# A hybrid encoder step: four gate columns regrouped into two seven-product units, and attention's side work moved between engines

## The chip, the cores and the metric

The kernel runs on one core of a Trainium2 chip. The core has TensorE (matrix products, PE in the profile), VectorE (DVE), ScalarE (ACT), GpSimd (POOL), SyncE (SP, which here issues most of the transfers) and 16 DMA engines. The metric is device time in microseconds for one launch; the time before is the median of three runs.

## The reference

One encoder layer is computed for 1024 prompt tokens and 32 sample tokens, so 1056 in all, at width 1024. The parts that matter here:

```
h = RMSNorm(x)
z = h @ W_in -> [q_A | k_A | v_A | q_B | f_B | i_B | og_B | gate_A | gate_B]
A: sliding-window attention over chunks of 64 frames, 16 query heads, 2 kv heads of width 64,
   a sink logit for each head, a shared relative-position bias
B: gated linear recurrence (HGRN2), 8 heads, key and value width 128
m = sigmoid(gate_A) * (y_A @ W_brA) + sigmoid(gate_B) * (y_B @ W_brB)
x = x + RMSNorm(m @ W_out)
x = x + ConvFFN(RMSNorm(x));  x = x + (p @ W_ple) * sigmoid(x @ W_ple_gate)
```

gate_A and gate_B are 1024 columns each, so 16 columns of 128 (the kernel's column), each a product of all 1056 tokens with a 1024 x 128 slice of W_in. Nothing in the mathematics says when they are computed: they are needed only in m.

## The kernel before

**Precision.** Every large product works on pairs. A value is split into a rounded high part and a low part, the rest. Three matmuls (high x high, high x low, low x high) are added up in PSUM; that is `product`, lines 200 to 202. A weight column of 1024 x 128 is loaded into a `wr` tile, and `load_next` makes `wh` and `wl` of it (lines 181 to 184). The list `hi_on` says whether ScalarE or VectorE makes the high part.

**A column.** The tokens lie in three groups of 384, 384 and 288 (`GR`). `unit(out)` gives three blocks of one column, one for each group, 24 matmuls each. `stream(blocks, small)` runs blocks one after the other in two halves of 12 matmuls, and after half number m it emits the small work that is filed under m in the dictionary `small`. `gate_out` puts a tanh on the finished block (line 292) and stores it to DRAM (`ta_d`, `tb_d`). `next_w` prepares weights two columns ahead of their use; the order of all columns is the list `plan`.

**Who sets the order.** A scheduler in the framework orders each engine's instructions with the program's order as priority. Work whose inputs or buffers are not ready in its planning is overtaken by later work. `pinned` and `behind` tie a piece of work to what its engine has been given last. Each engine, and each of the queues of SP and GpSimd, then runs strictly in that order.

**The stages around the change.**

- *Start.* The tokens are normalised, transposed and split into `La` and `Lb` (high and low part of h).
- *Attention* (`stream(blocks, small)` behind the loop over i). Eight pairs of query heads, i from 0 to 7, called head 1 to 8 here. For each, 9 token tiles j run through `scores` (line 451 on: matmuls with q and k, the sum with the bias and the minimum on VectorE, line 457, the exponential on ScalarE, line 462, the scaling by the reciprocal on VectorE, line 466), `turn` (transposition on TensorE, line 478, and a split, lines 223 and 224) and `values` (matmuls with v, lines 500 and 501; two copies by ScalarE and two adds by VectorE bring the high and low halves together, lines 507 to 510). A small copy by GpSimd (line 455) puts the sink into the score tile before the exponential. There are five score tiles. The blocks under which this small work lies are those of 11 gate columns and of q for the next head pair: 57 blocks. `GB_AT` says with which heads the first three columns of gate_B go. `h_sums` adds up halves of h for the recurrent stage (lines 516 to 528) and stores them from GpSimd's queue. `cache_parts` loads the cached keys and values and splits them.
- *Between.* One gate column, `tb_d[3]`, in a stream of its own, while the sums of h come back (`TL`, `TH`).
- *Recurrent stage.* Eight heads with two units each: q and f, i and the output gate. A unit computes two columns at once with seven block products instead of eight for the 768 tokens of the first two groups (a Strassen-Winograd scheme: the four quarters of two weight columns and the halves of h are added up first, `b_parts`, and the products are combined afterwards, `e0` to `e10`), and directly for the third group. These are 11 pieces of 12 matmuls (lines 1006 to 1009): seven at 384 tokens and four at 288. `b_raw` loads two columns, `b_prepare` makes the parts (lines 931 to 944) three pieces ahead. The work of a head (`decay`, `factors`, `tile_in`, `tile_out`, `group_out`) is filed under the pieces with `at(m, ...)`; a head's tiles run under the next head's pieces.
- *Gate columns 5 to 8 of gate_B.* The list `tail`, 12 blocks. Eight of them run with the last head's tiles; the other four in the next stage, with the first loads of attention's output.
- *First branch product.* `load_split` loads attention's output from `ya_d` in 32 pieces and splits it into `Ra` and `Rb` (line 1340, 223, 224). Then 8 columns with 4 blocks of 264 tokens each follow (line 1380 for the evictions). After it come the second branch product, W_out, the ConvFFN and the last product, which the change leaves alone.

`back` reloads the parts of h whose memory the recurrent stage had taken; `more` lets the preparation of later columns begin. Both are filed under the last pieces of the recurrent stage.

Of the kernel before, what the change touches and what calls it, by code (L numbers as in the profile page):

```python
# [10 lines left out]
F32 = mybir.dt.float32  # L11
# [48 lines left out]
def layer_kernel(  # L60
# [83 lines left out]
    GA = [in_cols(5376 + c * P) for c in range(8)]  # L144
    GB = [in_cols(6400 + c * P) for c in range(8)]
    GB_AT = (0, 3, 7)
    for i in range(8):
        plan.append(GA[i])
        if i in GB_AT:
            plan.append(GB[GB_AT.index(i)])  # L150
        if i < 7:
            plan.append(in_cols((i + 1) * P))
    plan.append(GB[3])
    n_first = len(plan)
    plan += GB[4:]
# [17 lines left out]
    def load_next():  # L173
# [6 lines left out]
        if hi_on[0] == "act":  # L180
            S.copy(hi[:], raw[:])  # L181
        else:
            V.tensor_copy(hi[:], raw[:])
        V.tensor_tensor(lo[:], raw[:], hi[:].bitcast(F32), op=ALU.subtract)  # L184
        ready.append((hi, lo))

    hi_on = ["act"]
# [124 lines left out]
    with right("ap") as ap:  # L312
# [73 lines left out]

        def cache_parts():
            ck = ap.tile([P, P], F32, tag="kr", name="ck", bufs=2)
            dma(ck[:], flat(cache_win_k))
            t = tr_bank()  # L390
            E.transpose(t[:, 0:P], ck[:], ident[:])
            kt_ = ap.tile([P, GMAX], F32, tag="kt", name="ckt", bufs=2)
            S.copy(kt_[:, 0:P], t[:, 0:P])
            k_parts(kt_[:, 0:P], 1024, P)
            cv_ = ap.tile([P, P], F32, tag="kr", name="cv", bufs=2)
            dma(cv_[:], flat(cache_win_v))
            v_parts(cv_[:], P, 8)
# [45 lines left out]
        def scores(i, j):  # L443
# [21 lines left out]
            for h in range(2):  # L465
                V.tensor_scalar(sc[:m_, h, b0:e_], sc[:m_, h, b0:e_], st[:m_, 1, h:h + 1], None,
                                op0=ALU.mult)
# [21 lines left out]
        def values(i, js):  # L489
# [13 lines left out]
            u = aq.tile([P, 2, P], F32, tag="u", name=nm("u"), bufs=2)  # L503
# [3 lines left out]
            S.copy(u[0:64, :nx, :m_], o4[64:128, :, 0, :])  # L507
            S.copy(u[64:128, :nx, :m_], o4[0:64, :, 1, :])
            V.tensor_tensor(y3[0:64], o4[0:64, :, 0, :], u[0:64, :nx, :m_], op=ALU.add)
            V.tensor_tensor(y3[64:128], o4[64:128, :, 1, :], u[64:128, :nx, :m_], op=ALU.add)  # L510
# [3 lines left out]
        def h_sums(k):  # L514
# [3 lines left out]
            b11, b12, b21, b22 = (t[:] for t in hs)  # L518
            for t, (g, k_) in zip(hs, ((0, k), (1, k), (0, k + 4), (1, k + 4))):
                V.tensor_tensor(t[:], La[g][k_].bitcast(F32), Lb[g][k_].bitcast(F32), op=ALU.add)  # L520
            for part, t in zip(h_d, (La, Lb)):
                dma(part[:, k, :], t[1][k].bitcast(F32))
            V.tensor_tensor(b11, b11, b12, op=ALU.subtract)
            V.tensor_tensor(b12, b12, b22, op=ALU.subtract)
            V.tensor_tensor(b22, b22, b11, op=ALU.add)
            V.tensor_tensor(b21, b21, b22, op=ALU.subtract)
            for j, b in enumerate((b22, b12, b11, b21)):
                gdma(t_d[j][:, k, :], b)

# [9 lines left out]
        with tc.tile_pool(name="np", bufs=1, side="right", reuse_waits="tile") as np_:  # L539
# [267 lines left out]
            for k in range(2, 8):  # L807
# [8 lines left out]
                if k == 3:  # L816
                    load_raw()
                if k == 5:
# [26 lines left out]
        blocks, small = [(lambda w=w: w, 2, out) for w, out in zip(ws, outs)], {}  # L845
        for i in range(8):
            lo_ = 2 * len(blocks) if i else 0
            blocks += unit(gate_out(ta_d[i]))
            if i in GB_AT:
                blocks += unit(gate_out(tb_d[GB_AT.index(i)]))  # L850
            if i < 7:
                blocks += unit(q_out(i + 1))
            hi_ = 2 * len(blocks) - (6 if i == 7 else 0)
            if i == 0:
# [6 lines left out]
                small.setdefault(28, []).append(lambda: hi_on.__setitem__(0, "dve"))  # L861
            if i < 7:
                small.setdefault(lo_ + 2, []).insert(0, lambda i=i: bias_load(i + 1))
            for m, k in {0: ((16, 0), (22, 1)), 3: ((4, 2), (12, 3))}.get(i, ()):
                small.setdefault(lo_ + m, []).append(lambda k=k: pinned(lambda: h_sums(k), V))
# [1278 lines left out]
```

## Time and profile before

| | us |
|---|---|
| median of the runs shown (lowest to highest) | 2001.23 (2001.19 to 2003.25) |
| the profiled execution | 2002.58 |
| its span, first to last instruction | 2000.8 |
| TensorE busy in the span | 1984.3 |
| VectorE busy | 1424.5 |
| ScalarE busy | 965.4 |
| GpSimd busy | 228.4 |

The span is what the profile's rows add up to; the 1.8 us around it belong to the execution but to no instruction. Matmuls overlap each other, so a matmul's own duration is longer than its share of TensorE's time; the distance from one start to the next is what counts. "L200" is line 200 of the kernel. In a row of a group, the shape, the count, the busy time and the mean duration in ns of one are followed by the idle time of the engine just before these instructions and by what ended it. In a row of a stretch stand, for each engine, the busy time and in brackets the number of instructions, in the order PE, PEld (weight loads of TensorE), DVE, ACT, POOL, and then the granted clock of TensorE, the mean busy share of the DMA engines and GB/s.

### The profile page before, as it was taken

To read this page: it belongs to the slowest core of one execution; us is meant where nothing else is said; L and a number is where in the kernel's file an instruction comes from. 1 tells how busy PE (TensorE), PEld (TensorE's weight loads), DVE (VectorE), ACT (ScalarE), POOL (GpSimd) and SP (SyncE) were. 2 spreads that over 40 slices of the span, in tenths; PEclk is the share of its full clock that TensorE was granted. 3 is DMA by queue.
4 is the path that set the end of the run, shared out by engine and by line. 5 is a ranking of instruction groups with operands and counts; after the bars stand their busy time and mean duration, and the time that the engine had idled before them with its cause. 6 is when DMAs were issued, how large, how long until landed. Compare 5 with 4: busy or idle time off the path is not lost.

```text
span 2000.8 us, 37359 instructions
## 1 busy us (share of the span) xinstructions
PE 1984.3 (99%) x14304; PEld 1955.0 (98%) x14304; DVE 1424.5 (71%) x3138; ACT 965.4 (48%) x2159; POOL 228.4 (11%) x323
## 2 busy tenths in 40 slices
PE   8999999999999999999999999999999999999998
PEld 7899999999999999999999999999999999999998
DVE  6788888688888888554455788788888784655552
ACT  7555566566666666442124663333333344444432
POOL 1110100000000000002001023333333210000000
PEclk9999999999999999999999999999999999999999
DMA  7622311411111111377558582222222245655543
GB/s 257 155 92 85 106 53 55 154 43 58 58 37 51 41 54 54 123 241 220 166 165 291 173 288 70 80 76 86 76 86 76 86 141 195 213 192 173 171 130 80
DMA packets 253639, 247.47 MB, mean 124 GB/s; under 512 B 13893, under 2 KB 221912, under 8 KB 253461
## 3 DMA queue, kind: packets, MB, share of 16 engines
q1 hardware_dynamic: 245141, 218.59, 35.3%
q0 software_dynamic: 8240, 26.44, 3.7%
q8 instruction: 112, 1.84, 0.4%
q14 instruction: 66, 0.54, 0.1%
q10 hardware_dynamic: 80, 0.07, 0.0%
HBM read 177.56 MB, written 65.32 MB: 121 GB/s over the span
## 4 chain that ended last, share of the span: by engine, by line
PE 92%; DVE 4%; ACT 2%; DMA 1%; issue 1%; POOL 0%; SPq 0%; DVEq 0%; ACTq 0%; POOLq 0%
PE mm L200 14%; PE mm L201 14%; PE mm L202 14%; PE st L1867 7%; PE st L1866 7%; PE st L1865 7%; PE G L1009 2%; PE Y L1006 2%; PE G L1008 2%; PE G L1006 2%; PE Y L1009 2%; PE Y L1008 2%; PE tr L478 1%; PE X L1006 1%; PE so L1200 1%; PE X L1009 1%
## 5 line engine op out<-in xcount | busy, mean ns | idle before, releaser
L1865 PE MATMUL st<-op,wt 128*128 128x264 f32 x1232 | 348.6, 283 | 2.0 <-DVE Sp L1878 1.3
L1867 PE MATMUL st<-op,wt 128*128 128x264 f32 x1232 | 349.8, 284 | 0.0
L1866 PE MATMUL st<-op,wt 128*128 128x264 f32 x1232 | 347.6, 282 | 0.0
L184 DVE TENSOR_TENSOR wl<-wr,wh 128x1024 fp32r<-128x1024 f32 x129 | 157.9, 1224 | 120.7 <-ACT wh L181 111.7
L1865 PEld LDWEIGHTS st<-op,wt 128*128 128x128 f32 x1232 | 231.2, 188 | 3.5 <-DVE Sp L1878 1.7
L1866 PEld LDWEIGHTS st<-op,wt 128*128 128x128 f32 x1232 | 231.4, 188 | 0.0
L1867 PEld LDWEIGHTS st<-op,wt 128*128 128x128 f32 x1232 | 230.9, 187 | 0.0
L181 ACT CAST wh<-wr 128x1024 fp32r<-128x1024 f32 x116 | 121.8, 1050 | 197.7 <-PE mm L201 136.1
L200 PE MATMUL mm<-La,wh 128*128 128x384 f32 (+1 forms) x528 | 174.4, 331 | 0.0
L201 PE MATMUL mm<-Lb,wh 128*128 128x384 f32 (+1 forms) x528 | 170.9, 324 | 0.6 <-DVE Lb L710 0.6
L200 PE MATMUL mm<-ac,wh 128*128 128x352 f32 x528 | 170.8, 323 | 0.0
L202 PE MATMUL mm<-La,wl 128*128 128x384 f32 (+1 forms) x528 | 170.5, 323 | 0.2 <-DVE wl L685 0.2
L202 PE MATMUL mm<-ac,wl 128*128 128x352 f32 x528 | 169.8, 322 | 0.0
L201 PE MATMUL mm<-ac,wh 128*128 128x352 f32 x528 | 169.3, 321 | 0.0
L1625 ACT CAST wt<-wu 128x512 fp32r<-128x512 f32 x126 | 77.9, 619 | 186.6 <-POOL ab L1851 88.3
L200 PE MATMUL mm<-Ra,wh 128*128 128x264 f32 x512 | 145.4, 284 | 0.0
L201 PE MATMUL mm<-Rb,wh 128*128 128x264 f32 x512 | 145.0, 283 | 0.0
L202 PE MATMUL mm<-Ra,wl 128*128 128x264 f32 x512 | 145.0, 283 | 0.0
L1626 DVE TENSOR_TENSOR wt<-wu,wt 128x512 fp32r<-128x512 f32 x126 | 103.0, 820 | 39.0 <-ACT wt L1625 39.0
L462 ACT ACTIVATE sc<-sc,st 128x257 f32<-128x257 f32 (+1 forms) x144 | 69.7, 485 | 74.0 <-DVE st L457 73.0
L201 PEld LDWEIGHTS mm<-Lb,wh 128*128 128x128 f32 x528 | 99.4, 188 | 1.7 <-DVE Lb L710 1.4
L202 PEld LDWEIGHTS mm<-La,wl 128*128 128x128 f32 x528 | 99.2, 188 | 0.7 <-DVE wl L685 0.5
(496 smaller groups left out, 5694.8 us busy)
## 6 DMA issues: line engine op xcount, KB each, us to landing
wr<-in_w_down_dram SPq DMA_DIRECT2D x66, 512.0 KB
wu<-in_w_up_dram SPq DMA_DIRECT2D x42, 512.0 KB
wu<-in_w_in_dram SPq DMA_DIRECT2D x32, 512.0 KB
wr<-in_w_in_dram SPq DMA_DIRECT2D x25, 512.0 KB
ac<-act_d SPq DMA_DIRECT2D x66, 176.0 KB
act_d<-Up SPq DMA_DIRECT2D x21, 528.0 KB
wr<-in_w_out_dram SPq DMA_DIRECT2D x16, 512.0 KB
pw_d<-pw POOLq DMA_DIRECT2D x11, 512.0 KB, 5.6
```

What stands on the lines that cost most here:

```text
L181: S.copy(hi[:], raw[:])
L184: V.tensor_tensor(lo[:], raw[:], hi[:].bitcast(F32), op=ALU.subtract)
L200: E.matmul(ps, wh, a, start=first and n == 0, stop=False)
L201: E.matmul(ps, wh, b, start=False, stop=False)
L202: E.matmul(ps, wl, a, start=False, stop=last and n == len(ks) - 1)
L1006: E.matmul(o, wh, x[0][k], start=first and k == 0, stop=False, skip_group_check=True)
L1008: E.matmul(o, wh, x[1][k], start=False, stop=False, skip_group_check=True)
L1009: E.matmul(o, wl, x[0][k], start=False, stop=k == 3, skip_group_check=True)
L1626: V.tensor_tensor(t[:, 1], src, t[:, 0].bitcast(F32), op=ALU.subtract)
L1865: E.matmul(o, wh, xh, start=first and k == 0, stop=False, skip_group_check=True)
L1866: E.matmul(o, wh, xl, start=False, stop=False, skip_group_check=True)
L1867: E.matmul(o, wl, xh, start=False, stop=k == 3, skip_group_check=True)
```

## The change

Sixteen gate columns stay sixteen, in a new order, and four of them are computed in another way.

- Attention runs with nine gate columns instead of eleven. `G_AT` deals their 27 blocks out to the eight heads, six to the first, two to the second, four to the last. From the second head on, q of the next head comes ahead of the gate blocks. Attention has 51 blocks instead of 57. The last head's small work is filed under four halves instead of six, and the values of tile 8 two halves later.
- The column between is `tb_d[1]`.
- Columns 2 to 5 of gate_B (counted from 0) become two units in the recurrent stage, one behind head 4 and one behind head 8 (`G_AFTER`, `gate_unit`), in the way that the heads' units are computed. A unit needs a place for one combination: `gu`, at the end of the tile `cb`.
- Two gate columns are left for `tail`: three blocks with the last head's tiles and three in the next stage.
- In attention, from half 28 on, a weight's high part is made by ScalarE. ScalarE also writes its negation to the low part's tile, and an accumulating transfer on GpSimd's queue adds the weight: 512 KB for each of the eleven weights from there on, the column between included. Before, VectorE made both parts there.
- The scaling of the second of two score tiles goes from VectorE to ScalarE, but for the first head.
- `values` copies both halves and both heads with one instruction of ScalarE on 128 partitions; the two adds read the copy across partitions.
- `h_sums` is cut into four steps and spread over heads 2, 3, 5 and 6, instead of running whole in heads 1 and 4.
- The cached keys and values are loaded before attention instead of inside it.
- `back` is filed two pieces later, and the last head's tiles and outputs a little later.

```diff
-    GB_AT = (0, 3, 7)
...
+    GATES = [(ta_d[c], 5376 + c * P) for c in range(8)] + [(tb_d[c], 6400 + c * P) for c in range(8)]
+    G_AT = (6,2,3,3,3,3,3,4)
+    N_A = sum(G_AT) // 3
...
-        if hi_on[0] == "act":
-            S.copy(hi[:], raw[:])
+        S.copy(hi[:], raw[:])
+        if lo_by[0] == "vector":
+            V.tensor_tensor(lo[:], raw[:], hi[:].bitcast(F32), op=ALU.subtract)
         else:
-            V.tensor_copy(hi[:], raw[:])
-        V.tensor_tensor(lo[:], raw[:], hi[:].bitcast(F32), op=ALU.subtract)
+            S.mul(lo[:], raw[:], -1.0)
+            gdma(lo[:], raw[:], accum_op=ALU.add)
...
+        def cache_load():
+            for src in (cache_win_k, cache_win_v):
+                cached.append(ap.tile([P, P], F32, tag="ck", name="ckv", bufs=2))
+                dma(cached[-1][:], flat(src))
...
-            for h in range(2):
-                V.tensor_scalar(sc[:m_, h, b0:e_], sc[:m_, h, b0:e_], st[:m_, 1, h:h + 1], None,
-                                op0=ALU.mult)
+            V.tensor_scalar(sc[:m_, 0, b0:e_], sc[:m_, 0, b0:e_], st[:m_, 1, 0:1], None, op0=ALU.mult)
+            if i:
+                S.mul(sc[:m_, 1, b0:e_], sc[:m_, 1, b0:e_], st[:m_, 1, 1:2])
...
-            S.copy(u[0:64, :nx, :m_], o4[64:128, :, 0, :])
-            S.copy(u[64:128, :nx, :m_], o4[0:64, :, 1, :])
-            V.tensor_tensor(y3[0:64], o4[0:64, :, 0, :], u[0:64, :nx, :m_], op=ALU.add)
-            V.tensor_tensor(y3[64:128], o4[64:128, :, 1, :], u[64:128, :nx, :m_], op=ALU.add)
+            S.copy(u[:, :nx, :, :m_], o4)
+            V.tensor_tensor(y3[0:64], o4[0:64, :, 0, :], u[64:128, :nx, 0, :m_], op=ALU.add)
+            V.tensor_tensor(y3[64:128], o4[64:128, :, 1, :], u[0:64, :nx, 1, :m_], op=ALU.add)
...
+            q = unit(q_out(i + 1)) if i < 7 else []
+            g = [of_gates.pop(0) for _ in range(G_AT[i])]
+            blocks += g + q if i == 0 else q + g
+            hi_ = 2 * len(blocks) - (4 if i == 7 else 0)
...
+    G_AFTER = {3: N_A + 1, 7: N_A + 3}
+    BU, unit_at = [], {}
     for h in range(8):
+        unit_at[h] = len(BU)
         BU += [(1280 + h * P, 2304 + h * P), (3328 + h * P, 4352 + h * P)]
+        if h in G_AFTER:
+            BU.append(tuple(GATES[G_AFTER[h] + a][1] for a in range(2)))
...
+        def gate_unit(h):
+            def out(dst):
+                def f(g, src):
+                    o, n = GR[g]
+                    t = gtile()
+                    S.activation(t[:, :n], src, AF.Tanh, scale=0.5)
+                    dma(dst[:, o:o + n], t[:, :n])
+                return f
+            a, b = (out(GATES[G_AFTER[h] + i][0]) for i in range(2))
+            return unit_pieces(unit_at[h] + 2, lambda: gu, a,
+                               lambda g: bt("x0", GMAX, 1)[:], b)
...
+            if h in G_AFTER:
+                pieces += gate_unit(h)
...
-                t_in = m1 + 2 + (j if last else j * 3 // 2)
+                t_in = m1 + 2 + (j * 5 // 4 if last else j * 3 // 2)
...
-        at(len(pieces) - 3, back)
+        at(len(pieces) - 1, back)
...
-        for c in range(4, 8):
-            u = unit(gate_out(tb_d[c]))
-            tail += [u[0], u[2], u[1]]
-        stream(tail[:8], {m - len(pieces): f for m, f in small.items()})
+        u, v = (unit(gate_out(dst)) for dst, _ in GATES[14:])
+        tail = [u[0], u[2], v[0], v[2], u[1], v[1]]
+        stream(tail[:3], {m - len(pieces): f for m, f in small.items()})
```

79 lines of the change are left out of this document (43 added, 36 removed).

## The prediction

> **What bounds the kernel now.** I read the shares first, then a table of stretches that follows the stages, then the waits and the order in time where a stretch shows idle TensorE.
>
> ```profile
> PE 1984.3 (99%) x14304; PEld 1955.0 (98%) x14304; DVE 1424.5 (71%) x3138; ACT 965.4 (48%) x2159; POOL 228.4 (11%) x323
> ```
>
> TensorE (PE) is busy for 99% of the span, so the time can fall in two ways only: fewer TensorE cycles, or some of the last 16.5 us of idle. The granted clock is full everywhere, as the next rows show. In them each engine has its busy time, then PEclk, the DMA share and GB/s.
>
> ```profile
> 56.00:100.00 44.00, 42.59 (x279) 39.46 (x278) 31.74 (x106) 27.17 (x76) 9.88 (x27) 1.00 0.60 148
> 100.00:336.00 236.00, 236.00 (x1644) 233.12 (x1643) 194.94 (x607) 133.52 (x411) 22.25 (x94) 1.00 0.25 81
> 336.00:372.00 36.00, 35.18 (x248) 33.89 (x246) 25.96 (x93) 22.18 (x69) 1.58 (x8) 1.00 0.11 42
> 372.00:386.00 14.00, 13.95 (x89) 13.90 (x90) 9.31 (x15) 7.09 (x13) 0.00 (x0) 1.00 0.81 303
> 386.00:790.00 404.00, 403.41 (x2653) 393.50 (x2652) 338.94 (x913) 254.35 (x657) 0.00 (x0) 1.00 0.18 54
> 790.00:812.00 22.00, 22.00 (x145) 20.90 (x143) 21.88 (x79) 17.06 (x49) 0.00 (x0) 1.00 0.19 59
> 812.00:856.00 44.00, 43.49 (x287) 41.61 (x286) 18.43 (x61) 17.64 (x54) 0.00 (x0) 1.00 0.44 139
> 856.00:878.00 22.00, 22.00 (x150) 22.00 (x150) 13.39 (x33) 13.43 (x35) 0.00 (x0) 1.00 0.81 237
> 878.00:968.00 90.00, 90.00 (x748) 90.00 (x747) 36.53 (x78) 21.80 (x43) 18.02 (x33) 1.00 0.70 213
> ```
>
> Attention is 56 to 372, the lone gate column 372 to 386, the recurrent stage 386 to 812, the four gate columns after it 812 to 872, the first branch product from there. VectorE (DVE) is at 194.94/236 = 0.83 through attention and 0.84 in the recurrent stage, without a TensorE gap. So an engine at 0.83 does not hold TensorE in these loops. Only the starts and ends of stages show idle: 1.4 us before 100, 0.8 us after 336, 0.5 us in the gate columns.
>
> **The products: -4.2 us.** One gate column is two blocks of 384 tokens and one of 288, each 24 matmuls. Three block starts of the present gate columns:
>
> ```profile
> 860.05 0.33 PE L200 MATMUL Z<-La,wh 128*128 128x384 f32 x1
> 864.21 0.29 PE L200 MATMUL G<-La,wh 128*128 128x288 f32 x1
> 867.39 0.34 PE L200 MATMUL X<-La,wh 128*128 128x384 f32 x1
> ```
>
> A 384 block takes 864.21 - 860.05 = 4.16 us and a 288 block 3.18 us, so a column takes 11.50 and two take 23.00. A unit has seven products of 12 matmuls at 384 (half a block, 2.08 us each) and four pieces of 12 at 288 (1.59): 14.56 + 6.36 = 20.92. One unit saves 2.08, two save 4.16. All of it is on TensorE's own path, and TensorE is the path.
>
> Beside it each unit costs VectorE weight sums, splits and combinations:
>
> ```profile
> L932 DVE TENSOR_TENSOR wt<-wu,wt 128x512 fp32r<-128x512 f32 x93 | 62.6, 685 | 14.4 <-ACT wt L931 14.1
> L1034 DVE TENSOR_TENSOR tf<-tf,Z 128x384 f32<-128x384 f32 x8 | 4.4, 547 | 0.0
> ```
>
> That is 8 splits and 4 sums at about 0.685 and 5 combinations at 0.55, 11.0 us in at least 20.9 us of TensorE. It lies under that at a share lower than the 0.84 which the stage carries now, and takes the last head's end out of the stretch where VectorE is at 21.88 of 22. I cost it at nothing; without that cover it would be 11 us.
>
> **Attention: less cover, other engines.** The stage goes from 57 blocks to 51, two columns or 23 us less, some 293 us instead of 316. The rows that price what moves (busy, mean ns of one):
>
> ```profile
> L462 ACT ACTIVATE sc<-sc,st 128x257 f32<-128x257 f32 (+1 forms) x144 | 69.7, 485 | 74.0 <-DVE st L457 73.0
> L466 DVE TENSOR_SCALAR sc<-sc,st 128x256 f32<-128x256 f32 (+1 forms) x144 | 42.4, 334 | 1.5
> ```
>
> ```profile
> L223 ACT CAST ph<-tr 128x512 fp32r<-128x512 f32 x56 | 32.4, 583 | 11.3 <-PE tr L478 11.0
> L507 ACT COPY u<-o 64x256 f32<-64x256 f32 x32 | 11.8, 370 | 10.2 <-PE o L501 9.8
> L508 ACT COPY u<-o 64x256 f32<-64x256 f32 x32 | 11.7, 365 | 0.4
> L292 ACT ACTIVATE gt<-mm 128x384 f32<-128x384 f32 x22 | 10.4, 478 | 1.8 <-PE mm L202 1.5 <-PE o L500 0.3
> L181 ACT CAST wh<-wr 128x1024 fp32r<-128x1024 f32 x6 | 6.3, 1057 | 1.8 <-PE mm L201 1.3 <-DMA wr<-in_w_in_dram 0.5
> ```
>
> ```profile
> L184 DVE TENSOR_TENSOR wl<-wr,wh 128x1024 fp32r<-128x1024 f32 x19 | 23.3, 1224 | 0.7
> L183 DVE CAST wh<-wr 128x1024 fp32r<-128x1024 f32 x13 | 8.9, 687 | 0.1
> ```
>
> VectorE loses 13 casts at 0.687 (8.9), 13 low parts at 1.224 (15.9: two columns go, 11 become transfers) and 63 scalings at 0.334 (21.0): 252.6 - 45.8 = 206.8 us of 293, a share of 0.71. ScalarE (ACT) gains two passes for 11 weights at 1.057 (23.3; the negation has no row, the cast of the same shape is nearest) and 63 scalings at 0.485 (30.6, priced as the exponentials of that shape). It loses 32 x (0.370 + 0.365 - 0.583) = 4.9 on the value copy and six gate tanh, 2.7: 182.9 + 46.3 = 229.2, a share of 0.78. Both stay below the 0.83 that runs without gaps, so this costs nothing in the middle. The adds on the copied values and the sums of h keep their work; the sums only leave heads 1 and 4 for heads 2, 3, 5 and 6, 4.4 us of VectorE (eight operations near 0.55) in each.
>
> In the last head four blocks remain of six: 36.0 - 2 x 4.16 = 27.7 us of TensorE. ScalarE's 22.2 loses 0.9 and gains 9 x 0.485 = 4.4: 25.7, or 0.93. Some of its work will come after the last block. What covers that is the lone gate column, 11.5 us on TensorE, if its blocks are ordered ahead of the late values. There is one gap today, for VectorE:
>
> ```profile
> 359.06 0.63 PE L478 MATMUL tr<-ident,sc 128*128 128x128 f32 x4 [0.72 <-DVE pl L224]
> ```
>
> I bound this end by -0.8 (the gap gone with a lighter VectorE) and +3 (ScalarE's 25.7 starting some 3.5 us behind the first score, on 27.7, less its overlap; an estimate), and take 0: one such gap for another.
>
> Six blocks less are twelve places less where small TensorE work interrupts a column. The cached keys' transposition also shows what an interruption costs:
>
> ```profile
> 88.62 0.31 PE L391 MATMUL tr<-ident,ck 128*128 128x128 f32 x1 [0.91 <-DMA ck<-in_cache_win_k_dram]
> 88.76 0.60 PE L478 MATMUL tr<-ident,sc 128*128 128x128 f32 x4
> 89.28 0.33 PE L361 MATMUL tr<-ident,kt 128*128 128x128 f32 x1
> 89.37 0.42 PE L200 MATMUL mm<-La,wh 128*128 128x384 f32 x1
> 89.63 0.34 PE L201 MATMUL mm<-Lb,wh 128*128 128x384 f32 x1
> ```
>
> The first matmul behind a transposition holds 0.26 us instead of 4.16/24 = 0.17, 0.09 more. Twelve of these give 0 to 1.1; behind scores there is less, so I take -0.5. The wait of 0.91 for the cached keys goes, since both are now loaded before the stage, two more issues early on SP's queue. Next behind it are transpositions that wait for scaled scores; bounds 0 and -0.91, I take -0.9.
>
> **The accumulating transfer** has no row. Its nearest is another 512 KB transfer issued by GpSimd (POOL): median 6.0 us to landing, 9.1 at most.
>
> ```profile
> DMA to landing us min/median/max: 4.0/6.0/9.1
> ```
>
> A weight is prepared two columns ahead, six blocks, so over 23 us. Two passes of 1.06, a 9.1 us landing and twice that if the destination is read as well make 20.3. Hence 0, with the failure below as a rival.
>
> **The first branch product: +0.8 us.** Its 32 activation loads start when the recurrent stage's memory is free. Four gate blocks cover them now (855.8 to 871.6), three afterwards: 3.18 + 2 x 4.16 = 11.5, so 4.2 less. Rows of the loads with their splits, the wait that held ScalarE, and the last two splits:
>
> ```profile
> L1340 SPq DMA_DIRECT2D ld<-ya_d x32: 319/382/1052, 856.8 to 876.4; - x32
> L223 ACT CAST Ra<-ld x32: 401/412/417, 861.4 to 879.3; 128x264 fp32r<-128x264 f32 x32
> ```
>
> ```profile
> ACT wh L181 <- PE Y L201: 4.2, 1, 4.2
> ```
>
> ```profile
> 879.36 0.78 DVE L224 TENSOR_TENSOR Rb<-ld,Ra 128x264 fp32r<-128x264 f32 x2 [0.40 <-ACT Ra L223]
> ```
>
> ```profile
> 871.56 0.28 PE L200 MATMUL mm<-Ra,wh 128*128 128x264 f32 x1
> ```
>
> The last split ends at 880.1. The fourth block needs it at 871.56 + 3 x 24 x 90/748 = 880.2. So the slack is 0.1 and the upper bound 4.1. Against it, the first load is issued at 856.8 and the first cast stands at 861.4, because ScalarE sat in front of a weight cast until TensorE gave a buffer back. That cast belongs to a column which then starts before this place: about 2.2 us return, and one weight (1.06 on ScalarE, 1.22 on VectorE) leaves the stretch. 4.1 - 2.2 - 1.1 = 0.8. The reload of h moves behind the gate unit, past two pieces; the blocks that need it are now fifth and sixth in the tail, so it is hidden.
>
> **Sum:** -4.2 - 0.5 - 0.9 + 0 + 0.8 = -4.8 us. The profiled execution took 2002.58 us, 2000.8 of it span; the median of the runs is 2001.23, so 1996.4.
>
> **Rivals.** B, the gain is handed back: the activation loads cost their full 4.1 and the cached keys' wait only changes its releaser. -4.2 - 0.5 + 4.1 = -0.6, 2000.6. For it speaks the DMA share of 0.81 in 856 to 878; against it ScalarE's 4.2 us wait.
>
> C, slower: GpSimd's queue is held. Each accumulating transfer stands there until ScalarE has negated its weight; the small copies of the sink behind it (line 455) feed every exponential. Eleven holds that each cost TensorE 1.2 us make 13.2 - 4.8 = +8.4, 2009.6; it decides from 0.8 us each. For it: one queue in order, and ScalarE at 0.78. Against: scores run three half blocks, some 6 us, ahead of their transposition. The present transfers on that queue issue thus:
>
> ```profile
> L528 POOL DMA_DIRECT2D t_d<-hs x16: 539/539/573, 97.3 to 212.0; - x16
> ```
>
> [...]
>
> **Chances.** Forecast 0.53, B 0.29, C 0.18. Faster by over 0.2% (4 us, about what a measurement can tell from no change) 0.54, within it 0.29, slower 0.17. Range: every favourable bound gives -4.2 - 1.1 - 0.9 - 0.8 = -7.0; -8 for unlisted waits, 1993.0. Upward, 4.1 at the branch and 3 at attention's end on -4.2 give +2.9, 2004.1; C lies mostly beyond. The likeliest case alone: 1994 to 1998.
>
> **What would show it.** Right: the seven-product pieces fill some 42 us more and the columns' blocks 46 us less; attention lasts near 293 us with ScalarE near 0.78; no wait on cached keys. Wrong: TensorE waits ended by activation casts at the start of the branch product, by a value split around the last head, or exponentials released by GpSimd.

## The result, and the profile after

The changed kernel took 2004.51 us (median; 2002.10 to 2007.43), the kernel before beside it 2001.67 (2000.61 to 2003.50). The ratio is 1.0014, with a 95% interval of 1.0007 to 1.0020: 2.8 us slower, inside the 0.2% that were named as no change, and 0.4 us above the top of the range. The forecast was 4.8 us faster.

The profiled execution of the changed kernel took 2006.86 us with a span of 2005.1. Cut at the same marks (the first matmul of the first scores, of the first product of the recurrent stage, of the first and of the second branch product; "pieces" ends with the last half product of the recurrent stage), the two traces compare so, in us:

| stretch | before | after | difference |
|---|---|---|---|
| start, to the first score | 56.55 | 60.55 | +4.00 |
| attention and the lone column | 329.24 | 307.43 | -21.81 |
| pieces of the recurrent stage | 426.14 | 475.71 | +49.57 |
| gate columns behind it | 59.63 | 28.05 | -31.58 |
| first branch product | 92.80 | 94.81 | +2.01 |
| all behind it | 1036.48 | 1038.58 | +2.10 |

The third and fourth row belong together, since small work of the last head moved from one to the other: +17.99, where two units less two columns are 41.84 - 23.00 = +18.84. The second to fourth rows together give -3.82, where the forecast's terms for them (-4.2, -0.5 and -0.9) add up to -5.6. The first branch product is 2.01 longer and not 0.8. What the forecast did not have at all is 4.0 us in the start. The last row is this execution's own: another execution of the same kernel has 1035.84 there.

The engines' line of the page, then the table of stretches (span, then PE, PEld, DVE, ACT and POOL busy with their instructions, PEclk, DMA share, GB/s), both of the changed kernel:

```profile
PE 1983.4 (99%) x14280; PEld 1950.5 (97%) x14280; DVE 1407.9 (70%) x3081; ACT 1011.4 (50%) x2220; POOL 237.8 (12%) x334
```

```profile
20.00:30.00 10.00, 7.34 (x42) 6.79 (x41) 5.47 (x15) 6.96 (x16) 0.00 (x0) 0.97 0.69 203
30.00:40.00 10.00, 9.26 (x53) 8.86 (x52) 5.30 (x11) 6.09 (x14) 0.00 (x0) 0.86 0.68 195
60.00:353.00 293.00, 291.25 (x2016) 282.29 (x2014) 214.84 (x706) 214.60 (x588) 42.87 (x140) 1.00 0.38 105
```

The same first two stretches of the kernel before:

```profile
20.00:30.00 10.00, 9.95 (x63) 9.45 (x62) 6.52 (x15) 9.02 (x20) 0.00 (x0) 1.00 0.74 217
30.00:40.00 10.00, 9.26 (x59) 8.83 (x59) 6.83 (x13) 7.16 (x14) 0.00 (x0) 1.00 0.87 282
```

Two things are to be read here. Between 20 and 30 us TensorE lost 2.6 us of busy time. Between 30 and 40 it was as busy as before, with six matmuls fewer and a granted clock of 0.86. The order in time of the changed kernel shows what stood there (start, duration, engine, line, operation, and in brackets the idle time and what ended it):

```profile
26.70 0.30 ACT L345 CAST Vs<-ckv 128x128 fp32r<-128x128 f32 x1 [3.00 <-DMA ckv<-in_cache_win_v_dram]
26.91 1.15 ACT L586 ACTIVATE x<-x,n 128x1024 f32<-128x1024 f32 x1
27.03 0.29 DVE L346 TENSOR_TENSOR Vs<-ckv,Vs 128x128 fp32r<-128x128 f32 x1 [2.54 <-ACT Vs L345]
...
28.11 0.44 PE L597 MATMUL s<-ident,x 128*128 128x128 f32 x2 [2.42 <-ACT x L586]
```

Line 345 is the split of the cached values, which belongs to the first head of attention. It is in ScalarE's queue at 23.7 us, waits 3.00 us for the transfer, and the scaling of x behind it is what TensorE needs. The cached keys' wait of 0.91 us at 88 us is gone, as forecast; this one, earlier and dearer, came with it.

### The profile page after: what moved, and what is told of

Same layout as the page of the kernel before. It is cut to its first block, busy times and chain, and to the rows that moved or that the text cites. A ratio compares the mean times of both kernels' runs of the same rounds, so it can differ in the third digit from the quotient of the medians.

```text
span 2005.1 us, 37257 instructions
## 1 busy us (share of the span) xinstructions
PE 1983.4 (99%) x14280; PEld 1950.5 (97%) x14280; DVE 1407.9 (70%) x3081; ACT 1011.4 (50%) x2220; POOL 237.8 (12%) x334
## 4 chain that ended last, share of the span: by engine, by line
PE 88%; DVE 4%; DMA 3%; issue 2%; ACT 2%; SPq 1%; POOL 0%; DVEq 0%; ACTq 0%; POOLq 0%
PE mm L203 13%; PE mm L204 13%; PE mm L205 13%; PE st L1904 7%; PE st L1903 7%; PE st L1902 7%; PE Y L1031 2%; PE G L1034 2%; PE G L1031 2%; PE G L1033 2%; PE Y L1034 2%; PE Y L1033 2%; PE tr L487 1%; PE X L1031 1%; PE X L1034 1%
## 5 line engine op out<-in xcount | busy, mean ns | idle before, releaser
L182 ACT CAST wh<-wr 128x1024 fp32r<-128x1024 f32 x125 | 131.3, 1050 | 188.1 <-PE mm L204 135.3
L184 DVE TENSOR_TENSOR wl<-wr,wh 128x1024 fp32r<-128x1024 f32 x114 | 139.6, 1224 | 111.2 <-ACT wh L182 100.2
L203 PE MATMUL mm<-La,wh 128*128 128x384 f32 (+1 forms) x480 | 159.0, 332 | 0.0
L204 PE MATMUL mm<-Lb,wh 128*128 128x384 f32 (+1 forms) x480 | 155.9, 325 | 0.6 <-DVE Lb L723 0.4
L205 PE MATMUL mm<-La,wl 128*128 128x384 f32 (+1 forms) x480 | 155.5, 324 | 0.1
L203 PEld LDWEIGHTS mm<-ac,wh 128*128 128x128 f32 x528 | 99.0, 187 | 1.5 <-ACT sq L2023 1.0
L204 PEld LDWEIGHTS mm<-ac,wh 128*128 128x128 f32 x528 | 99.6, 189 | 0.0
L205 PEld LDWEIGHTS mm<-ac,wl 128*128 128x128 f32 x528 | 98.9, 187 | 0.0
```

What stands on the lines that cost most here:

```text
L203: E.matmul(ps, wh, a, start=first and n == 0, stop=False)
L204: E.matmul(ps, wh, b, start=False, stop=False)
L205: E.matmul(ps, wl, a, start=False, stop=last and n == len(ks) - 1)
```

## The experiments

Differences of some 2 us are near what can be told: the 95% intervals of the ratios below are about 1.8 us wide to either side. So each reading stands on a median and on the stretch of the trace that the edit touches. A difference of two kernels is that of their medians; where they were measured on different chips, the difference of their distances from the kernel before beside each is given too. Two more executions, of the kernel before and of the changed kernel, show how far stretches repeat.

> The kernel before once more, unchanged, for how far two profiled executions of one kernel lie apart. All theories expect the stretches from mark to mark (first score, first branch product, second branch product, end) within 0.5 us of the first profile's; the time was 2002.58 us in that profile and 2001.67 by the median, so up to 1.5 us may lie in stretches that no edit touches.

> The changed kernel once more, unchanged. Theory: the wait of ScalarE for the cached values at 26 us and TensorE's idle 2.2 to 2.7 us behind it come in every execution, the granted clock's fall behind it only in some; so the first score comes between 2 and 4 us later than the 56.55 of before. Rival: it is one accident of the first profile, and the start is that of before.

The kernel before gave 2003.2 us of span where its first profile had 2000.8. All of it lies in the second stretch (331.76, not 329.24): a value product's wait of 2.0 us for its cast at 82 us, with a granted clock of 0.83 behind it, neither of which the first execution has. The other stretches lie within 0.5 us (56.87, 426.16, 59.62, 92.80, 1035.99). So a single execution's second stretch is good to 2.5 us only where its waits are listed. The changed kernel gave 2000.9: ScalarE waited 1.24 us for the cached values and not 3.00, TensorE lost 0.8 us of busy time between 20 and 30 us (9.11 against 9.95), and the clock stayed at 1.00; its first score came at 57.85. The length of the wait changes from execution to execution, the wait comes in each.

**The start: where the cached values are split.** Three kernels. The first takes the early transfers back:

```diff
         def cache_parts():
+            cache_load()
             ck, cv_ = cached
...
                     load_raw()
-                    cache_load()
```

> The changed kernel with one edit taken back: the two transfers of the cached keys and values are issued where the cached keys are treated, behind the first query products, and no longer ahead of the stage. Theory: the early transfers let the split of the cached values (L345) run ahead into the start, where ScalarE stood 3.0 us for them, TensorE 2.42 us behind it, and the granted clock fell to 0.86 for 10 us; so the start falls back by 4.0 us (first score at 56.5 instead of 60.55), a wait of the cached keys of 0.9 us comes back, and the time is 3 to 4 us under the changed kernel's (about 2000.5 to 2001.5). Rival: the 4.0 us come from the new order of the blocks or from the sums' stores that run early in the queue; then the time stays within 1 us of the changed kernel's.

It took 2003.27 us, ratio 1.0008 (0.9999 to 1.0017), 1.2 us under the changed kernel and not 3 to 4. The edit did not do what it says: the transfers are still issued at 20.7 us, since their two buffers are free from the start and the program's order is only one of the things that place a transfer. In the kernel before they share their buffers (the tag "kr") with key rows, and that was what kept them late, at 86.7 us. So this kernel repeats the changed one, with a shorter wait:

```profile
L393 SPq DMA_DIRECT2D ckv<-in_cache_win_v_dram x1: 422/422/422, 21.2 to 21.2; - x1
```

```profile
25.84 0.30 ACT L345 CAST Vs<-ckv 128x128 fp32r<-128x128 f32 x1 [1.33 <-DMA ckv<-in_cache_win_v_dram]
```

The second keeps the early transfers and holds the work on them in its place on all three engines:

```diff
-                    small.setdefault(m, []).append(lambda f=f: pinned(f, E))
+                    es = (E, S, V) if f is cache_parts else (E,)
+                    small.setdefault(m, []).append(lambda f=f, es=es: pinned(f, *es))
```

> The changed kernel with its early transfers, but with the treatment of the cached keys and values held in its place on ScalarE and VectorE too, and not on TensorE alone. Theory of the split moved ahead: ScalarE no longer waits at 26.7 us, TensorE's granted clock stays at 1.00 through the start, and the time is 4 to 5 us under the changed kernel's (about 1999.5 to 2000.5), some 0.9 under the kernel with late transfers, since the keys are there when they are turned. Rival, the early transfers' own place in the queue delays the inputs of the start: the 3 us wait moves to another transfer of the start, and the time stays within 1 us of the changed kernel's.

2001.27 us, ratio 0.9996 (0.9987 to 1.0005), 3.2 us under the changed kernel. The split now stands at 85.3 us and the start is as before:

```profile
20.00:30.00 10.00, 9.95 (x63) 9.50 (x61) 6.95 (x16) 9.14 (x20) 0.00 (x0) 1.00 0.76 217
30.00:40.00 10.00, 9.26 (x60) 8.79 (x59) 6.42 (x12) 7.48 (x15) 0.00 (x0) 1.00 0.87 278
```

The third is the kernel before with nothing but the early transfers (the same `cache_load`, called in the start, two buffers "ck"):

> The kernel before with this one part of the change alone: the cached keys and values are loaded ahead of the stage into buffers of their own. Theory of the split moved ahead: the same wait of ScalarE at about 26 us, the same fall of the granted clock, and 3 to 4 us more than the kernel before (0.9 of it given back at the cached keys). The prediction's reading: 0.9 us less than the kernel before.

2003.64 us, ratio 1.0011 (1.0002 to 1.0020): 1.8 us slower, by one part of the change that the forecast had at -0.9. Its first score comes at 60.61 us, 4.06 later than before:

```profile
26.76 0.30 ACT L342 CAST Vs<-ckv 128x128 fp32r<-128x128 f32 x1 [3.08 <-DMA ckv<-in_cache_win_v_dram]
```

With the split held in its place, the same part alone shows what the wait at the cached keys was worth:

> The kernel before with the early transfers of the cached keys and values, and their treatment held in its place on ScalarE and VectorE: the cached keys' wait is taken away and the start left as it was. Prediction's step: 0.9 us under the kernel before. Rival (the wait is a cover for something that comes late anyway, or is made up in most executions): the same time as before within 0.3 us.

2000.84 us, ratio 0.9996 (0.9987 to 1.0004): 0.6 us under the kernel before, by its median; the second stretch falls from 329.24 to 328.28. The size of the forecast (0.9) fits, though the interval holds nothing too. By these two kernels the split in the start costs 1.8 + 0.6 = 2.4 us; by the changed kernel and its held form it was 3.4, each taken against the kernel before beside it. In the traces with the split in the start ScalarE's wait is 1.24 to 3.08 us long, and the granted clock from 30 to 40 us is 0.83 to 1.00; the size differs from execution to execution.

**The branch products.** The changed kernel's waits between 866 and 895 us have TensorE waiting for the activations' parts:

```profile
ACT Ra L226 <- DMA ld<-ya_d: 5.3, 7, 1.6
PEld mm L204 <- DVE Rb L227: 0.8, 3, 0.3
PEld mm L203 <- ACT Ra L226: 0.6, 3, 0.3
```

With the split held, one column was moved from attention to the tail, so that four blocks cover the loads again:

```diff
-    G_AT = (6,2,3,3,3,3,3,4)
+    G_AT = (6,2,2,3,3,3,2,3)
...
-        tail = [u[0], u[2], v[0], v[2], u[1], v[1]]
-        stream(tail[:3], {m - len(pieces): f for m, f in small.items()})
+        tail = [u[0], u[2], v[0], v[2], u[1], v[1], w_[0], w_[2], w_[1]]
+        stream(tail[:5], {m - len(pieces): f for m, f in small.items()})
```

> The changed kernel with the treatment of the cached values held in its place, and one gate column moved from the attention stage to the blocks behind the recurrent stage, so that four blocks stand between the first load for the branch products and the branch products, as in the kernel before, and not three. The number of blocks and units stays. Theory (the lead is what the branch products lack): the remainders of their first eight inputs are ready 8.8 us ahead as before and not 6.9, the first branch product falls from 94.4 to 92.8 us, and the time is 1.6 us under the kernel with the held treatment alone (about 1999.7). Rival (the loads are late because the transfers are slow): 94.4 us stays, and the time with it, 2001.3.

The first branch product fell to 92.91 us as the theory has it, and yet the kernel took 2005.01 us, ratio 1.0016 (1.0008 to 1.0025). The casts of the early loads now stand in ScalarE's queue ahead of the gates' tanh, and TensorE waits for the bank that it empties; the pieces of the recurrent stage grew too, from 475.74 to 478.65. In this trace three products there wait 0.9 us each, one for a half sum of h (`TH`) and two for VectorE's combinations (L1053); the kernel with the held split has one such wait, of 0.6 us. Why they come is not shown. So the theory holds for its own stretch, and the time was lost elsewhere.

```profile
PE mm L203 <- ACT gt L295: 1.9, 1, 1.9
```

The other way is more buffers for the same loads:

```diff
-        t = mt("ld", 8)
+        t = mt("ld", 15)
```

> The changed kernel with the treatment of the cached values held in its place, and with 15 buffers for the loads ahead of the branch products, not 8. Theory (the lead is short and the transfer engines are near full, busy 0.86 in this stretch): nothing is to be had from buffers, the first branch product stays at 94.4 us. Rival (a load waits for its buffer until a cast and a subtraction free it): the loads are issued earlier, the remainders come earlier, and up to 1.6 us come back.

1999.19 us, ratio 0.9988 (0.9979 to 0.9997), 2.1 under the kernel with the held split (1.5 by the distances from the kernel before), and the first branch product is back at 92.80. The rival of the expectation holds: a load did wait for its buffer. The loads' lines, first of the changed kernel, then of this one in its second execution:

```profile
L1377 SPq DMA_DIRECT2D ld<-ya_d x32: 319/382/1934, 861.2 to 880.9; - x32
```

```profile
L1378 SPq DMA_DIRECT2D ld<-ya_d x32: 376/410/1261, 857.7 to 875.2; - x32
```

All 32 are issued within 17.5 us instead of 19.7. That is 2 us. In the second execution the first branch product takes 93.08 us, so the products lack 0.3 us at most. This kernel, with the held split and 15 buffers, is called the mended kernel below. It was run again beside the next ones:

> The kernel with the held treatment and 15 load buffers once more, so that the three kernels beside it are compared on one chip: 1999.2 expected, 2.1 us under the kernel before.

1998.94 us, ratio 0.9986 (0.9977 to 0.9995): 2.5 us faster than the kernel before.

**The units.** Two kernels have fewer. The first has one, on the kernel with the held split; eleven columns lie in attention:

```diff
-    G_AT = (6,2,3,3,3,3,3,4)
+    G_AT = (6,3,4,4,4,4,4,4)
...
-    G_AFTER = {3: N_A + 1, 7: N_A + 3}
+    G_AFTER = {7: N_A + 1}
```

> The changed kernel with the treatment of the cached values held in its place, and with one unit of two gate columns (in the last head) and not two; the other two columns are done as plain blocks in the attention stage, eleven there as before. Prediction's step: a unit takes 20.92 us and its two columns as blocks 23.00, so this is 2.08 us above the kernel with two units and the held treatment (about 2003.3 by its median of 2001.27), with the stretch from the first score to the first branch product 2.1 longer. Rival (the attention stage cannot hide its work with nine columns and its price is in the stage): the eleven columns give some of the 2.08 back, and the difference is under 1 us.

2004.11 us, ratio 1.0013 (1.0004 to 1.0021): 2.8 above the kernel with two (3.4 by the distances from the kernel before). The way from the first score to the first branch product is 815.54 us against 810.70, so 4.8 and not 2.1. In this trace value products wait 3.7 us together, once for a cast of scores that stands behind a weight's cast in ScalarE's queue (L182, 80.15 to 81.19 us), and three times for something that ended with the negation of a weight (what it is, follows under "Attention's edits"):

```profile
PE o L509 <- ACT ph L226: 1.9, 1, 1.9
PE o L509 <- ACT wl L186: 1.8, 3, 1.1
```

The second is the mended kernel with no unit (`G_AFTER = {}`, eleven columns in attention, four in the tail in the old order):

> The kernel with the held treatment and 15 load buffers without the two units: eleven gate columns in the attention stage, one behind it and four behind the recurrent stage, all as plain blocks in the order of the kernel before; the other edits stay. Prediction's step: the two units are worth 4.16 us, so this is 4.2 above the kernel with units, 2003.4, and the stretch from the first score to the first branch product is 4.2 longer. Rival (the units give part of it back in the recurrent stage, or the shorter attention stage does): the difference is 2 us or less, and the missing part lies in the units; if the difference is 4.2, it lies in the other edits.

2004.78 us, ratio 1.0016 (1.0007 to 1.0024), 5.8 above the mended kernel beside it. Pieces and tail together are 485.63 us without units and 503.88 with them, +18.25; two columns less there are 23.00 and two units 41.84, which is +18.84. The second stretch is 331.77 without and 307.92 with, -23.85, where two columns are 23.00. So the units are worth what their products say, 4.16, and about 0.6 and 0.85 more. And the kernel without them, in which only the other edits and the 15 buffers are left, is 3.3 us slower than the kernel before.

**Attention's edits.** With the split held, the branch loads mended and no units, what is left lies in attention's stretch: 331.77 us, where the kernel before with the early transfers held has 328.28. Four kernels undo parts. Value products copied crossed in two steps as before, with the held split:

```diff
-            S.copy(u[:, :nx, :, :m_], o4)
+            S.copy(u[0:64, :nx, :m_], o4[64:128, :, 0, :])
+            S.copy(u[64:128, :nx, :m_], o4[0:64, :, 1, :])
```

> The changed kernel with the treatment of the cached values held in its place, and with the value products copied in two steps, crossed between the halves of the partitions, as before. The waits of the value products (L509) for VectorE's sums (L518), 0.7 us in three, are new in the changed kernel. If the one-step copy makes them, they go and the time is about 1 us under the kernel with the held treatment alone; if the scaling on ScalarE or the shorter stretch of blocks makes them, they stay and the time is the same or, with more work on ScalarE (some 36 copies more), up to 1 us longer.

2001.73 us, ratio 1.0001 (0.9992 to 1.0009), 0.5 above the kernel that it is made from (1.0 by the two ratios). The waits for the sums of the values did not go; they grew from 0.7 us in three to:

```profile
PE o L509 <- DVE ya L519: 1.7, 5, 0.7
```

So the copy in one step doesn't make these waits. Scaling of both halves on VectorE, on the mended kernel:

> The kernel with the held treatment and 15 load buffers, with both halves of the scores scaled on VectorE as before. If the scaling on ScalarE relieves the stage, this is 1 to 2 us above 1999.2; if it makes the value products wait (ScalarE's queue between the exponentials and the copies), 1 us below; the prediction has it at 0.

2001.07 us, ratio 0.9998 (0.9989 to 1.0007), with single runs from 1998.4 to 2006.6. The median is 1.9 above the mended kernel's (1.4 by the distances from the kernel before), as the first reading of the expectation has it, but the trace puts none of that in attention: the way from the first score to the first branch product is 811.61 us (811.80 in the mended kernel). The profiled execution's excess is 0.8 at the first branch product and some 4 us far behind it, at 1154 us (last section). So whether the scaling on ScalarE brings anything stays open; in its own stage this trace shows nothing. The remainders of attention's weights by VectorE, twice, on the changed and on the mended kernel (`lo_by` stays "vector"):

> The changed kernel with the remainders of the attention stage's weights taken by VectorE to the end, so that no transfer adds into a tile. The prediction put this part at 0: then the time is within 1 us of the changed kernel's, VectorE's share in the attention stage going from 0.73 to about 0.76 and ScalarE's from 0.72 to about 0.68. Rival (the queue of GpSimd is held by these transfers and the blocks come late): the time falls by some us.

> The kernel with the held treatment and 15 load buffers, the remainders of the attention stage's weights taken by VectorE to the end. Prediction's step: 0, within 0.5 us of the kernel with transfers (1999.2). Rival C, GpSimd's queue held: it is faster. The other way: VectorE is short of time in a stage of nine columns and the value products wait more, 1 to 2 us slower.

2004.92 us (1.0016; 1.0007 to 1.0025), 0.4 above the changed kernel, and 1999.95 (0.9992; 0.9983 to 1.0001), 1.0 above the mended one beside it, with the second stretch 309.08 against 307.92. The accumulating transfers are no burden; what they bring, 1.0 us at most by these medians, is within the noise. Their landing (min, median, max), by the row of line 187 of the changed kernel:

```profile
L187 POOL DMA_DIRECT2D wl<-wr x11: 852/873/926, 118.7 to 309.7; - x11
...
DMA to landing us min/median/max: 4.6/4.8/7.7
```

Last, the mended kernel with the whole of attention's work divided as before (casts and remainders of weights on VectorE, crossed copies, both scalings on VectorE):

> The kernel with the held treatment and 15 load buffers, with the attention stage's work divided over the engines as before: from the second head on VectorE copies and subtracts each weight, no transfer adds into a tile, value products are copied crossed in two steps, both halves of the scores are scaled on VectorE. The units, the nine columns and the spread sums stay. Prediction's reading: these edits cost nothing and bring at most 1 us, so the time is that of the kernel with all of them, 1999.2, or 1 us above. Rival (nine columns don't hide the old division): the time is several us above, 2003 or more, VectorE's share of the attention stage at or above 0.85.

2003.02 us, ratio 1.0005 (0.9996 to 1.0014), 3.3 above the mended kernel when each is taken against the kernel before beside it. The steady part of the stage, 150 to 350 us, in four kernels: before with held early transfers (eleven columns, old division), no units (eleven, new division), mended (nine, new division), and this one (nine, old division).

```profile
150.00:350.00 200.00, 200.00 (x1396) 197.30 (x1396) 164.14 (x526) 115.66 (x359) 16.84 (x74) 1.00 0.23 75
```

```profile
150.00:350.00 200.00, 198.12 (x1371) 194.73 (x1370) 133.44 (x437) 140.68 (x379) 28.29 (x87) 1.00 0.40 108
```

```profile
150.00:350.00 200.00, 198.89 (x1397) 194.04 (x1396) 147.99 (x488) 152.73 (x420) 27.36 (x90) 1.00 0.35 98
```

```profile
150.00:350.00 200.00, 196.72 (x1376) 191.67 (x1375) 171.52 (x557) 120.33 (x373) 22.83 (x81) 1.00 0.22 74
```

The old division with eleven columns leaves TensorE no idle at a VectorE share of 164.14/200 = 0.82. The new one with eleven columns idles 1.9 us although neither engine is above 140.68/200 = 0.70. The longest waits there:

```profile
PE o L509 <- ACT wl L186: 1.8, 3, 1.0
```

The view puts a wait for several things down to the one that ended last, here the negation of a weight (L186). A value product does not read that weight. The order in time of the longest of the three shows what it needs (ScalarE, VectorE and TensorE, in part):

```profile
162.37 1.03 ACT L182 CAST wh<-wr 128x1024 fp32r<-128x1024 f32 x1
...
164.41 0.19 ACT L516 COPY u<-o 128x64 f32<-128x64 f32 x1
164.50 1.06 ACT L186 ACTIVATE wl<-wr 128x1024 fp32r<-128x1024 f32 x1
164.93 0.35 DVE L472 TENSOR_SCALAR sc<-sc,st 128x256 f32<-128x256 f32 x1
165.29 0.19 DVE L518 TENSOR_TENSOR ya<-o,u 64x32 f32<-64x32 f32 x1
...
165.63 0.36 PE L509 MATMUL o<-ph,Vs 128*128 128x256 f32 x1 [1.04 <-ACT wl L186]
```

The value products have one PSUM bank, `o`, and VectorE's second add (L518) empties it 0.15 us before the product starts. Of ScalarE's work nothing but the negation ends between the copy (L516, at 164.60 us) and the product. In the mended kernel the view names this add itself (0.7 us in three). The add stands behind a scaling in VectorE's queue (L472). The copy that it reads (L516) stands in ScalarE's queue behind two exponentials and the cast of a weight, 1.03 us, which VectorE made before. So several operations stand in front of the one that TensorE needs, although both engines have room.

With nine columns the old division has VectorE at 0.86 and idles 3.3 us, the new one 1.1. So the new division is needed once two columns have left. The price of all of attention's edits together, in the second stretch, is 331.77 - 328.28 = 3.5 us with eleven columns (3.9 by the medians); with nine it is 307.92 - (328.28 - 23.00) = 2.6 us. Only part of the 3.5 is idle time of TensorE: over the two second stretches that is 2.8 us (331.77 - 328.95 busy) against 1.7 (328.28 - 326.59). In the rest TensorE counts as busy, at wider distances between matmuls: in the rows above (150 to 350 us) 1371 recorded ones take 198.12 us without units, and 1396 take 200.00 in the kernel before with held early transfers, 0.1445 us each against 0.1433. Which edit makes it is not shown: the kernel without units also has the new order of the blocks and the spread sums of h, and no run has these with the old division and eleven columns.

## Why the prediction was wrong

| term | forecast | measured | by |
|---|---|---|---|
| units and fewer interruptions | -4.7 | -5.8 | mended kernel against no units, medians |
| cached keys' wait | -0.9 | -0.6 | early transfers alone, held |
| attention's other edits together, division of work among them | 0 | +3.5 | no units against early transfers held, second stretch |
| first branch product | +0.8 | +1.6 to +2.0 | 94.40 (held split) and 94.81 (changed) against 92.80 |
| split of the cached values in the start | not in the sum | +3.4 | changed against held split, each against the kernel before beside it |
| sum | -4.8 | +2.1 to +2.5 | the change measured +2.8 |

The products, the seven-product pieces and their place on TensorE's path are right, and the stage's end around the last head, taken at 0 between -0.8 and +3, has no gap left in the changed kernel (TensorE is busy for 21.94 of the 22 us from 350 to 372). The accumulating transfers at 0 hold within 1 us: a landing of 7.7 us at most against the 9.1 that the forecast allowed. Rival C falls with that: no exponential was released by GpSimd, and without these transfers the kernel is not faster.

Three steps failed.

**"The wait of 0.91 for the cached keys goes, since both are now loaded before the stage, two more issues early on SP's queue."** The wait went. But the step counted two issues, and left out every instruction that a load releases. `pinned` held the treatment of the cached tiles on TensorE alone. On ScalarE and VectorE the split of the values was kept late by nothing but its late load, and with the load early it was placed in the start, in front of the scaling of x. The sum lacks 3.4 us for it, and this alone reverses the sign: without it the measured terms add up to some -1, and the kernel with the held split is at 0.9996.

**"Both stay below the 0.83 that runs without gaps, so this costs nothing in the middle."** The shares came out near the forecast, 214.84/293 = 0.73 for VectorE (0.71) and 214.60/293 = 0.73 for ScalarE (0.78). The inference is what fails: a stage at 0.82 on one engine ran without a gap, and one with 0.67 on VectorE and 0.70 on ScalarE did not. A share tells how much room an engine has. It does not tell where the one operation that TensorE waits for stands in its engine's queue: in the waits seen it was the add that empties the value products' bank, behind a scaling, with exponentials and a weight's cast of 1.03 us in front of the copy that it needs. These waits are 1.8 us. Attention's edits together cost 2.6 (nine columns) to 3.5 us (eleven) and not 0, and the cause of the rest stays open. The new division by itself saves 3.3 us against the old one at nine columns.

**The branch loads' +0.8.** The mechanism is right (TensorE waiting for activation parts at the start of the branch products), and the size is half of the 1.6 to 2.0. Of the credits, the 2.2 us for ScalarE's wait in front of a weight cast (which has no working) and the 1.1 us for a weight less, not enough came: the first load is issued 10.5 us ahead of the first product (861.2 to 871.73), where it was 14.8. What was missing is the buffers. With eight, a load is issued only when a cast and a subtraction have freed one, so that the late start can't be made up; with 15 it can. In the changed kernel the queue waits for such a subtraction in 15 loads, 6.0 us together; with 15 buffers that is 4.2 us in 14.

Rival B had the branch at its full 4.1 us and the gain handed back there, 2000.6 us. Its effect is seen and half of its size, and its time is not that of the result; the gain was handed back in the start and in attention too. The range's lower end comes out at 1993.2 by its own sum, not 1993.0; nothing hangs on it.

## What to carry to other kernels

When a transfer is moved early, ask which instructions were waiting for nothing else: they move too, into whatever queue they stand in, and a wait there blocks all that is behind (here 3.00 us of ScalarE, and 2.42 us of TensorE behind it). Hold them where they were (here one line gave some 3 us back), or leave the buffers shared that kept the load late. And don't price moved work by the engine's share alone: look for the one operation that TensorE waits for next, and for what stands in front of it in its queue.

## What the runs showed of the hardware

Short idle times of TensorE cost more than their length here in one execution (2.42 us, a start 4.0 us longer) and not in another (2.01 us, 2.1 us longer). Behind the 2.42 us of the changed kernel the matmuls at 384 stand 0.32 us apart (29.19, 29.52, 29.84) and from 32.9 us 0.17 again:

```profile
29.19 0.53 PE L203 MATMUL mm<-La,wh 128*128 128x384 f32 x1
29.52 0.52 PE L204 MATMUL mm<-Lb,wh 128*128 128x384 f32 x1
29.84 0.52 PE L205 MATMUL mm<-La,wl 128*128 128x384 f32 x1
```

The changed kernel without accumulating transfers has a gap of 2.01 us in the same place and no fall of the clock; its start is 2.1 us longer and not 4.0:

```profile
27.81 0.44 PE L597 MATMUL s<-ident,x 128*128 128x128 f32 x2 [2.01 <-ACT x L586]
```

```profile
20.00:30.00 10.00, 7.76 (x46) 7.20 (x45) 5.88 (x15) 7.36 (x17) 0.00 (x0) 1.00 0.69 202
30.00:40.00 10.00, 9.25 (x62) 8.82 (x61) 6.20 (x13) 7.53 (x17) 0.00 (x0) 1.00 0.84 252
```

So about half of the 4.0 us is the wait, and half the clock behind it. From 29.35 to 32.76 us the granted clock of the changed kernel is 0.50: 3.41 us at half rate, 1.7 us of work. The falls in the kernel before with the early transfers alone (30.01 to 33.43 us; 0.83 from 30 to 40) and in the second execution of the kernel before (82.75 to 86.16, behind 2.0 us of idle; 0.83 from 80 to 90) are as long. One is twice as long, 1155.28 to 1162.11 us, in the kernel with both scalings on VectorE. A gap of 0.84 us stands before it, between matmuls of one column each (128x1). The granted clock there:

```profile
1150.00:1154.00 4.00, 3.50 (x34) 3.42 (x33) 4.00 (x8) 2.49 (x7) 0.77 (x1) 1.00 0.97 327
1154.00:1160.00 6.00, 5.65 (x33) 5.65 (x34) 2.77 (x16) 0.60 (x1) 1.49 (x2) 0.61 0.99 332
1160.00:1170.00 10.00, 10.00 (x78) 10.00 (x78) 5.14 (x5) 3.92 (x8) 2.35 (x4) 0.89 0.37 132
```

The length of the idle time alone does not tell when the clock falls: it fell behind 2.42 and 2.0 us, and once soon after 0.84 us, and stayed at 1.00 behind 2.01 us. What makes it fall is not shown.
